# Absolute values on ScalarE instead of VectorE in an encoder layer's sigmoids, softplus and attention

## The chip, the cores and the metric

The kernel runs on one core of one Trainium2 chip. The core has five engines that run side by side, each in its own order of instructions: TensorE (PE in the profile, its weight loads PEld), VectorE (DVE), ScalarE (ACT), GpSimd (POOL) and SyncE (SP), which issues most of the transfers. The metric is the device time of one execution in microseconds, lower is better.

## The reference

One layer of a streaming encoder is applied to 1024 prompt frames and 64 sample frames with the same weights, in fp32. The parts that the change touches are these:

```python
z = jnp.where(mask, jnp.einsum('bhqd,bhnkd->bhqnk', qf[...], ki), SB_NEG)   # attention scores
sp = jax.nn.softplus(z)
c_in = jnp.einsum('bhqnj,js->bhqns', sp, upper)                            # running sums along the keys
a = jnp.exp(z - c_in - later[..., None])                                   # stick-breaking weights
outs.append(jnp.einsum('bhqnk,bhnkd->bhqd', a, vi))

qkv = jax.nn.silu(causal_depthwise(full, conv_w))                          # sigmoids: delta rule, its gate,
a = u[..., :GROUP_W] * jax.nn.sigmoid(u[..., GROUP_W:])                    # conv module (twice),
ffn = (jax.nn.silu(h2 @ ffn_w_gate) * (h2 @ ffn_w_up)) @ ffn_w_down        # feed-forward
g = -jnp.exp(a_log) * jax.nn.softplus(u_a + dt_bias)                       # decays of the delta rule
```

Around them stand a modulation from a condition vector, RMS norms, one input projection, four mixers (a convolution of 31 taps, a gated delta rule in chunks of 64, pooling, attention), an output projection and a SwiGLU feed-forward net.

## The kernel before, in words

The frames are cut into half A (512 prompt frames) and half B (512 prompt frames and the 64 sample frames). Features lie on the 128 partitions, frames along the free dimension. Every large product is done three times with operands that are split into a rounded part and a remainder (`hi`, `lo`, and `whi`, `wlo` for weights): `load_w` fetches a weight tile (`wraw`), ACT rounds it (`whi`, L117), DVE subtracts (`wlo`, L123), and `gemm_fm` issues the matmuls (`pg`, L141). The program is written in this order: `in_proj(HA)`, `mixers(HA)`, `in_proj(HB)`, `mixers(HB)`, `out_proj(HA)`, `ffn(HA)`, `out_proj(HB)`, `ffn(HB)`. A scheduler then lays the instructions of each engine out in a fixed order of its own, from a model of their durations and from priorities, so that one half's matrix products fill in where the other half's mixers wait. A small edit can therefore move instructions of every engine. Each engine then runs its list strictly in order, and an instruction that waits holds up all behind it.

Softplus and sigmoid are built from one table set that has both the exponential and the logarithm: softplus(z) = max(z, 0) + ln(1 + exp(-|z|)). The absolute value is taken by DVE, which clears the sign bit (`vabs`, L134 and L135), then ACT does the exponential and the logarithm (L114), then DVE adds the maximum (L126).

`sb_block` (from L446) handles one block of attention scores, at most 128 keys by 512 queries. There are 16 blocks for half A (4 heads of 4), 32 for half B and 2 for the sample frames. PE writes the scores to the only bank of tag `z`. ACT copies them to `zs` (three buffers), DVE writes their absolute value to `e` (one buffer), ACT does the exponential and the logarithm on `e`, DVE adds the maximum. The sum is split into `sh` (ACT) and `sl` (DVE), PE multiplies both with a triangle (`u_r`) into `psC`, DVE subtracts that from `zs`, ACT takes the exponential, PE adds the other triangle (`omu_r`) to `psC` for the next block and multiplies by the values into `psO`. For half B the weights are split again into `ph` and `pl`.

`sigmoid_chain` (from L183) is used for the delta rule's features and gate (`dne`, `ge`), the convolution's input and output (`cve`, `cvz`), 14 feed-forward tiles of half A (`fe`) and once at the start. The later feed-forward tiles use ACT's Silu, which needs another table set. `dn_decays` has a softplus of its own (`abl`).

`dn_group` (from L702) does four chunks of the delta rule at a time, twice for each half, and once for the sample frames. It begins with `pgcb`, then `pkk` and `pkq` (products of keys and queries); DVE makes `nl` from `pkk`. `nl` goes out to DRAM (`nld`), comes back in another layout (`fsn`), POOL solves triangles of 16 rows (`fst`, `fsu`), the result goes out (`xd`) and comes back as `X`. Only then can PE do the transposes `pw`, and the chain of the four chunks after them.

Of the kernel before, what the change touches and what calls it, by code (L numbers as in the profile page):

```python
# [9 lines left out]
I32 = mybir.dt.int32  # L10
ACTF = mybir.ActivationFunctionType
ALU = mybir.AluOpType
# [47 lines left out]
def hybrid_encoder_kernel(ctx: ExitStack, tc: tile.TileContext, io):  # L60
    nc = tc.nc
# [46 lines left out]
    def PZ(name):  # L108
        return ps_sb.tile([P, 512], F32, tag="z", name=name)
# [3 lines left out]
    def act_(out, in_, func, bias=0.0, scale=1.0):  # L113
        nc.scalar.activation(out, in_, func, bias=bias, scale=scale)  # L114

    def copy_a(out, in_):
        nc.scalar.activation(out, in_, ACTF.Copy)  # L117

    def copy_v(out, in_):
        nc.vector.tensor_copy(out=out, in_=in_)  # L120

    def tt(out, a, b, op):
        nc.vector.tensor_tensor(out=out, in0=a, in1=b, op=op)  # L123

    def stt(out, a, s, b, op0, op1):
        nc.vector.scalar_tensor_tensor(out, a, s, b, op0, op1)  # L126
# [4 lines left out]
        else:  # L131
            nc.vector.tensor_scalar(out, a, s1, s2, op0, op1)

    def vabs(out, a):  # L134
        nc.vector.tensor_scalar(out.bitcast(I32), a.bitcast(I32), 0x7FFFFFFF, None, ALU.bitwise_and)  # L135

    def ptt(out, a, b, op):
        nc.gpsimd.tensor_tensor(out=out, in0=a, in1=b, op=op)  # L138

    def mm(out, lhsT, rhs, start=True, stop=True):  # L140
        return nc.tensor.matmul(out, lhsT=lhsT, rhs=rhs, start=start, stop=stop)  # L141

    def mms(out, lhsT, rhs, start=True, stop=True):
        nc.tensor.matmul(out, lhsT=lhsT, rhs=rhs, start=start, stop=stop, skip_group_check=True)  # L144

    def f(ap):
        return ap.bitcast(F32)
# [7 lines left out]
    def C(name):  # L155
        o, w = CONST_COLS[name]
        return cst[:, o:o + w]

    def V(name, i=None, n=1):
        o, w = VEC_COLS[name]  # L160
        if i is None:
            return vec[:, o:o + w]
        return vec[:, o + i:o + i + n]
# [17 lines left out]


    def sigmoid_chain(e, a):  # L183
        vabs(e, a)
        act_(e, e, ACTF.Exp, scale=-1.0)
        act_(e, e, ACTF.Ln, bias=1.0)
        stt(e, a, 0.0, e, ALU.min, ALU.subtract)
        act_(e, e, ACTF.Exp)
# [8 lines left out]
    def ada_setup():  # L197
        t = sm.tile([P, KT, 2], F32, tag="c2t", name="c2t", bufs=1)
        sigmoid_chain(t, c2)
        tt(c2, c2, t, ALU.mult)  # L200
        cb = [sb.tile([P, 1024], F32, tag=f"cb{g}", name=f"cb{g}") for g in range(2)]
        for g in range(2):
            for x in range(2):
                d = TT("cdiag")[:, 0:512]
                tt(d.rearrange("p (k c) -> p k c", c=P), C("ident").unsqueeze(1).to_broadcast([P, 4, P]),
                   c2[:, 4 * x:4 * x + 4, g:g + 1].to_broadcast([P, 4, P]), ALU.mult)
                pb = PD("pcb")
                mm(pb, C("ones"), d)
                copy_a(cb[g][:, 512 * x:512 * x + 512], pb)
            cbt.append(cb[g])  # L210
# [236 lines left out]
    def sb_block(rows, wid, zmm, psC, psO, kpart, first, last, avs, rounded=True):  # L447
        z = PZ("z")
        zmm(z)
        zs = sb.tile([P, 512], F32, tag="zs", name="zs", bufs=3)  # L450
        e = sb.tile([P, 512], F32, tag="e", name="e")
        r = slice(rows, 128)
        copy_a(zs[r, 0:wid], z[r, 0:wid])
        vabs(e[r, 0:wid], zs[r, 0:wid])
        act_(e[r, 0:wid], e[r, 0:wid], ACTF.Exp, scale=-1.0)
        act_(e[r, 0:wid], e[r, 0:wid], ACTF.Ln, bias=1.0)
        stt(e[r, 0:wid], zs[r, 0:wid], 0.0, e[r, 0:wid], ALU.max, ALU.add)
        sh = sb.tile([P, 512], F32R, tag="sh", name="sh")
        sl = sb.tile([P, 512], F32R, tag="sl", name="sl")
        copy_a(sh[r, 0:wid], e[r, 0:wid])  # L460
        tt(sl[r, 0:wid], e[r, 0:wid], f(sh[r, 0:wid]), ALU.subtract)
        o = 512 - wid if psC is not None and kpart else 0
        mms(psC[:, o:o + wid], u_r[r], sh[r, 0:wid], first, False)
        mms(psC[:, o:o + wid], u_r[r], sl[r, 0:wid], False, False)
        tt(zs[r, 0:wid], zs[r, 0:wid], psC[r, o:o + wid], ALU.subtract)
        act_(zs[r, 0:wid], zs[r, 0:wid], ACTF.Exp)
        if not last:
            mms(psC[:, o:o + wid], omu_r[r], sh[r, 0:wid], False, False)
            mms(psC[:, o:o + wid], omu_r[r], sl[r, 0:wid], False, False)
        if not rounded:  # L470
            for i, (v, out, c0) in enumerate(avs):
                n = out.shape[-1]
                mms(out, v, zs[r, c0:c0 + n], first and i == 0, last)
            return
        ph = sb.tile([P, 512], F32R, tag="ph", name="ph")
        copy_a(ph[r, 0:wid], zs[r, 0:wid])
        pl = sb.tile([P, 512], F32R, tag="pl", name="pl")
        tt(pl[r, 0:wid], zs[r, 0:wid], f(ph[r, 0:wid]), ALU.subtract)
        for i, (v, out, c0) in enumerate(avs):
            n = out.shape[-1]  # L480
            mms(out, v, ph[r, c0:c0 + n], first and i == 0, False)
            mms(out, v, pl[r, c0:c0 + n], False, last)
# [149 lines left out]
    def dn_decays(h):  # L632
        NC = 9 if h.samp else 8
        ab = abt[h.name]
        v = dn.tile([P, 2, 2, 9], F32, tag="abv", name="abv")
        nt = 5 if h.samp else 4
        for par in range(2):
            n_t = nt if par == 1 else 4
            pe = ps_dn.tile([P, 512], F32, tag="dn", name="psel")
            rp = slice(64 * par, 64 * par + 64)  # L640
            mm(pe[:, 0:8 * n_t], C("sel2")[rp], ab[rp, 0:n_t].rearrange("p t c -> p (t c)"))
            src = pe[:, 0:8 * n_t].rearrange("p (t a q b) -> p a q t b", a=2, q=2, b=2)
            for hp in range(2):
                r = slice(64 * hp, 64 * hp + 64)
                for a in range(2):
                    copy_v(v[r, a, :, par:8:2], src[r, a, :, 0:4, hp])
                    if n_t == 5:
                        copy_v(v[r, a, :, 8:9], src[r, a, :, 4:5, hp])
        vv = v[:, :, :, 0:NC]
        tt(vv[:, 0], vv[:, 0], V("dtb").unsqueeze(2).to_broadcast([P, 2, NC]), ALU.add)  # L650
        l = dn.tile([P, 2, 2, 9], F32, tag="abl", name="abl")
        ll = l[:, :, :, 0:NC]
        vabs(ll, vv)
        act_(ll, ll, ACTF.Exp, scale=-1.0)
        act_(ll, ll, ACTF.Ln, bias=1.0)
        D = {}
        for nm in ("g", "lnb", "gc", "kd", "gl", "beg", "beta"):
            D[nm] = dn.tile([P, 2, 9], F32, tag=f"c_{nm}", name=f"c_{nm}")[:, :, 0:NC]
        ea = sm.tile([P, 2], F32, tag="ea", name="ea", bufs=1)
        act_(ea, V("alog"), ACTF.Exp)  # L660
        stt(D["g"], vv[:, 0], 0.0, ll[:, 0], ALU.max, ALU.add)
        stt(D["g"], D["g"], -1.0, ea.unsqueeze(2).to_broadcast([P, 2, NC]), ALU.mult, ALU.mult)
        stt(D["lnb"], vv[:, 1], 0.0, ll[:, 1], ALU.min, ALU.subtract)
        pg = ps_dn.tile([P, 512], F32, tag="dn", name="pgc")
        mm(pg[:, 0:2 * NC], C("bdu"), D["g"])
        mm(pg[:, 64:64 + 2 * NC], C("bdones"), D["g"])
        copy_v(D["gc"], pg[:, 0:2 * NC].rearrange("p (a c) -> p a c", a=2))
        tot = pg[:, 64:64 + 2 * NC].rearrange("p (a c) -> p a c", a=2)
        tt(D["kd"], tot, D["gc"], ALU.subtract)
        act_(D["kd"], D["kd"], ACTF.Exp)  # L670
        act_(D["gl"], tot, ACTF.Exp)
        act_(D["beta"], D["lnb"], ACTF.Exp)
        tt(D["lnb"], D["gc"], D["lnb"], ALU.add)
        act_(D["beg"], D["lnb"], ACTF.Exp)
        D["gcl"] = D["lnb"]
        return D
# [663 lines left out]
def build(nc):  # L1340
    io = {}
    for n, s in _IN_SHAPES:
        io[n] = nc.dram_tensor(f"in_{n}_dram", s, F32, kind="ExternalInput").ap()
    for n, s in _OUT_SHAPES:
        io[n] = nc.dram_tensor(f"out_{n}_dram", s, F32, kind="ExternalOutput").ap()
    with tile.TileContext(nc, schedule_with_timeline_sim=True) as tc:
        hybrid_encoder_kernel(tc, io)
# [10 lines left out]
```

## Time and profile before

| | |
|---|---|
| median of 3 runs | 1543.53 us (1539.69 to 1544.31) |
| the profiled execution, its own time | 1542.9 us |
| its span, first to last instruction | 1541.1 us |
| busy: PE, PEld | 1467.3 us, 1263.4 us |
| busy: DVE, ACT, POOL | 1056.2 us, 626.8 us, 87.4 us |
| mean granted TensorE clock | 0.949 |

The span is cut into stages for reading. A busy time of PE that equals a stage's length means that matmuls follow one another; matmuls are pipelined, so a busy PE need not be at its peak. The granted clock stands as a share of full speed (1.00 is 2.4 GHz). Idle time of an engine is listed with what ended it.

### The profile page before, as it was taken

The page shows a single profiled execution, that of the slowest core. Times are in us where ns is not written, and L with a number is a line of the kernel's source. Part 1 is how long each engine was busy: PE and PEld are TensorE (multiplying, and loading weights), DVE is VectorE, ACT ScalarE, POOL GpSimd, SP SyncE. Part 2 cuts the span into 40 slices and gives each one's busy share as a digit, 9 for nine tenths or more (in the row PEclk, how much of TensorE's full clock was granted, in tenths as well). Part 3 has the DMA queues.
Part 4 walks back from the last instruction along what each step waited for, and adds up shares of the span by engine and source line. Part 5 has one row for each costly group of instructions (what it writes and reads, how often), then busy time and mean ns, then how long its engine had stood idle before and what let it go on. Part 6 is the DMA issues. An engine that isn't in the chain of part 4 may idle for free.

```text
span 1541.1 us, 24527 instructions
## 1 busy us (share of the span) xinstructions
PE 1467.3 (95%) x9688; PEld 1263.4 (82%) x9688; DVE 1056.2 (69%) x1911; ACT 626.8 (41%) x1096; POOL 87.4 (6%) x196
## 2 busy tenths in 40 slices
PE   7999999968998989899999989999999999999999
PEld 5777899745896867587777767789899999999998
DVE  8887799857488998776777588744655455555554
ACT  4446444535543566465566442222432222222221
POOL 0001300030003000300300000000000000000000
PEclk8999799958997999799999999999999999999999
DMA  8787577231555223242323478632322222222222
GB/s 311 274 280 232 168 220 233 98 85 60 166 165 135 70 54 88 83 145 88 101 88 92 131 241 260 216 109 84 127 78 83 83 83 83 83 83 83 83 83 103
DMA packets 106866, 205.40 MB, mean 133 GB/s; under 512 B 39360, under 2 KB 49024, under 8 KB 106752
## 3 DMA queue, kind: packets, MB, share of 16 engines
q1 hardware_dynamic: 99936, 193.36, 39.0%
q0 software_dynamic: 6816, 10.49, 3.0%
q8 instruction: 76, 1.25, 0.3%
q14 instruction: 38, 0.31, 0.1%
HBM read 175.57 MB, written 28.24 MB: 132 GB/s over the span
## 4 chain that ended last, share of the span: by engine, by line
PE 73%; DMA 9%; DVE 9%; issue 3%; ACT 2%; POOL 2%; SPq 2%; DVEq 0%; ACTq 0%; POOLq 0%
PE pg L141 59%; DMA wads<-in_wadat_dram 3%; PE psC L144 2%; DVE junk L215 2%; PE pw L141 1%; PE psO L144 1%; DVE wlo L123 1%; PE z L144 1%; POOL fsu L138 1%; POOL fst L138 1%; DMA nld<-nl 1%; DMA X<-xd 1%; DVE xA L126 1%; DMA wadt<-in_wadat_dram 1%; DVE cy L126 1%
## 5 line engine op out<-in xcount | busy, mean ns | idle before, releaser
L141 PE MATMUL pg<-hi,whi 128*128 128x288 f32 (+1 forms) x1504 | 504.5, 336 | 8.6 <-ACT whi L117 4.2
L141 PE MATMUL pg<-hi,wlo 128*128 128x288 f32 (+1 forms) x1504 | 500.5, 334 | 5.5 <-DVE wlo L123 5.3
L141 PE MATMUL pg<-lo,whi 128*128 128x288 f32 (+1 forms) x1504 | 501.6, 334 | 1.9 <-DVE lo L126 1.9
L117 ACT ACTIVATE whi<-wraw 128x1024 fp32r<-128x1024 f32 (+2 forms) x192 | 199.4, 1040 | 503.2 <-PE pg L141 442.1
L141 PEld LDWEIGHTS pg<-hi,whi 128*128 128x128 f32 x1504 | 286.6, 191 | 37.1 <-ACT whi L117 5.8
L141 PEld LDWEIGHTS pg<-hi,wlo 128*128 128x128 f32 x1504 | 286.3, 190 | 30.4 <-DVE wlo L123 7.6
L141 PEld LDWEIGHTS pg<-lo,whi 128*128 128x128 f32 x1504 | 286.9, 191 | 29.2 <-issue 4.2
L123 DVE TENSOR_TENSOR wlo<-wraw,whi 128x1024 fp32r<-128x1024 f32 (+2 forms) x192 | 230.3, 1200 | 97.6 <-ACT whi L117 95.8
L141 PE MATMUL pg<-g,whi 128*128 128x288 f32 (+1 forms) x1056 | 253.9, 331 | 5.5 <-DVE xA L126 5.0
L141 PEld LDWEIGHTS pg<-g,whi 128*128 128x128 f32 x1056 | 178.5, 189 | 22.8 <-DVE xA L126 6.9
L141 PE MATMUL pg<-g,wlo 128*128 128x288 f32 (+1 forms) x528 | 172.8, 329 | 0.0
L126 DVE SCALAR_TENSOR_TENSOR xs<-pg,mod,xs 128x288 f32<-128x288 f32 (+2 forms) x288 | 106.4, 412 | 85.7 <-PE pg L141 82.6
L141 PEld LDWEIGHTS pg<-g,wlo 128*128 128x128 f32 x528 | 99.6, 189 | 7.8
L123 DVE TENSOR_TENSOR fa<-fa,pg 128x288 f32<-128x288 f32 (+1 forms) x66 | 35.0, 531 | 100.0 <-PE pg L141 96.6
L126 DVE SCALAR_TENSOR_TENSOR cy<-cvb,vec,cy 128x512 f32<-128x512 f32 (+1 forms) x120 | 94.0, 793 | 0.2
L126 DVE SCALAR_TENSOR_TENSOR xA<-pg,mod,xA 128x512 f32<-128x512 f32 x96 | 70.3, 745 | 15.5 <-PE pg L141 15.3
L114 ACT ACTIVATE e<-e 128x512 f32<-128x512 f32 (+4 forms) x100 | 51.5, 515 | 39.0 <-DVE e L135 37.7
L215 DVE CUSTOM_DVE_ANT_0 junk<-wads,cb,vec 128x1024 bf16<-128x1024 f32 x32 | 41.0, 1282 | 14.7 <-DMA wads<-in_wadat_dram 14.5
L141 PE MATMUL pg<-mixs,whi 128*128 128x288 f32 x256 | 50.9, 295 | 0.0
L215 DVE CUSTOM_DVE_ANT_0 junk<-wadt,cb,vec 128x1024 bf16<-128x1024 f32 x32 | 40.9, 1278 | 11.6 <-DMA wadt<-in_wadat_dram 11.6
L141 PEld LDWEIGHTS pg<-mixs,whi 128*128 128x128 f32 x256 | 41.0, 188 | 0.1
L114 ACT ACTIVATE zs<-zs 128x512 f32<-128x512 f32 (+4 forms) x50 | 25.7, 514 | 34.5 <-DVE zs L123 34.4
(305 smaller groups left out, 1920.6 us busy)
## 6 DMA issues: line engine op xcount, KB each, us to landing
wraw<-in_wgate_dram SPq DMA_DIRECT2D x44, 512.0 KB, 3.6
wraw<-in_wup_dram SPq DMA_DIRECT2D x44, 512.0 KB, 3.8
wraw<-in_wdown_dram SPq DMA_DIRECT2D x44, 512.0 KB, 3.7
wadt<-in_wadat_dram SPq DMA_DIRECT2D x32, 512.0 KB, 4.6
wads<-in_wadat_dram SPq DMA_DIRECT2D x32, 512.0 KB, 4.2
wraw<-in_wfm_dram SPq DMA_DIRECT2D x30, 512.0 KB, 4.6
wraw<-in_wout_dram SPq DMA_DIRECT2D x16, 512.0 KB, 3.8
xA<-in_xa_dram SPq DMA_DIRECT2D x16, 256.0 KB, 5.5
```

Of the source, the lines that this page charges most:

```text
L114: nc.scalar.activation(out, in_, func, bias=bias, scale=scale)
L117: nc.scalar.activation(out, in_, ACTF.Copy)
L123: nc.vector.tensor_tensor(out=out, in0=a, in1=b, op=op)
L126: nc.vector.scalar_tensor_tensor(out, a, s, b, op0, op1)
L138: nc.gpsimd.tensor_tensor(out=out, in0=a, in1=b, op=op)
L141: return nc.tensor.matmul(out, lhsT=lhsT, rhs=rhs, start=start, stop=stop)
L144: nc.tensor.matmul(out, lhsT=lhsT, rhs=rhs, start=start, stop=stop, skip_group_check=True)
L215: nc.vector.tensor_tensor_reduce(out=junk, in0=w, in1=cbt[g], scale=1.0, scalar=V("b_ada", col), op0=ALU.mult, op1=ALU.add, accum_out=mod[ ...
```

## The change

Three places take the absolute value with ACT's Abs (by the helper `act_`, L114) instead of DVE's instruction: `sigmoid_chain`, the decays, and the attention. In the attention Abs reads the scores directly from PSUM, and the copy of the scores to `zs` is written behind the logarithm instead of in front of everything. `vabs` is gone, so the lines behind it have numbers smaller by three.

```diff
-    def vabs(out, a):
-        nc.vector.tensor_scalar(out.bitcast(I32), a.bitcast(I32), 0x7FFFFFFF, None, ALU.bitwise_and)
-
...
     def sigmoid_chain(e, a):
-        vabs(e, a)
+        act_(e, a, ACTF.Abs)
         act_(e, e, ACTF.Exp, scale=-1.0)
         act_(e, e, ACTF.Ln, bias=1.0)
         stt(e, a, 0.0, e, ALU.min, ALU.subtract)
...
         r = slice(rows, 128)
-        copy_a(zs[r, 0:wid], z[r, 0:wid])
-        vabs(e[r, 0:wid], zs[r, 0:wid])
+        act_(e[r, 0:wid], z[r, 0:wid], ACTF.Abs)
         act_(e[r, 0:wid], e[r, 0:wid], ACTF.Exp, scale=-1.0)
         act_(e[r, 0:wid], e[r, 0:wid], ACTF.Ln, bias=1.0)
+        copy_a(zs[r, 0:wid], z[r, 0:wid])
         stt(e[r, 0:wid], zs[r, 0:wid], 0.0, e[r, 0:wid], ALU.max, ALU.add)
...
-        vabs(ll, vv)
+        act_(ll, vv, ACTF.Abs)
         act_(ll, ll, ACTF.Exp, scale=-1.0)
```

The scheduler lays the program out anew. ACT, at the first attention blocks of half A (`zs` is the copy of the scores, `e` the block's softplus; the other names are other mixers' and projections' tiles). Before:

```order
L117 ACTIVATE zs_2410<-z_2406 128x128
L114 ACTIVATE cve_2835<-cve_2835 128x512
L117 ACTIVATE Y_1603<-pw0_1650 128x512
L117 ACTIVATE zs_2432<-z_2428 128x256
L117 ACTIVATE zs_2454<-z_2450 128x384
L114 ACTIVATE dne_1920<-dne_1920 128x512
L117 ACTIVATE vf_3031<-pv_2981 128x264
L114 ACTIVATE e_2411<-e_2411 128x128
```

Now:

```order
L114 ACTIVATE e_2411<-z_2406 128x128
L117 ACTIVATE zs_2410<-z_2406 128x128
L114 ACTIVATE cve_2835<-cve_2835 128x512
L114 ACTIVATE e_2411<-e_2411 128x128 x2
L117 ACTIVATE Y_1603<-pw0_1650 128x512
```

Before, three blocks' copies stood ahead of the first block's exponential. Now each block's Abs and copy stand as a pair, and the next block's pair comes after the exponential and logarithm of this one.

PE, at the second chunk group of half A, in front of the transposes of the solved triangle (`pw`); `psC` and `psO` are the attention's sums and outputs, `pvar` belongs to the convolution. Before:

```order
L141 MATMUL pvar<-cvs,cst 128x256 x2
L144 MATMUL psO<-zs,v_2594 64x256
L144 MATMUL psC<-sh,u_r 128x384
L144 MATMUL psC<-sl,u_r 128x384
L141 MATMUL pvar<-cvs,cst 128x256 x2
L731 MATMUL pw_2130<-cst,X 64x64
```

Now:

```order
L141 MATMUL psC<-sl,u_r 128x384
L141 MATMUL z<-q_2693,k_2691 128x128 x2
L141 MATMUL z<-neg_r,id_r 128x128
L141 MATMUL psC<-sh,omu_r 128x384
L141 MATMUL psC<-sl,omu_r 128x384
L141 MATMUL psO<-zs,v_2594 64x384
L141 MATMUL psC<-sh,u_r 128x512
L141 MATMUL psC<-sl,u_r 128x512
L728 MATMUL pw_2130<-cst,X 64x64
```

The rest of the 384-wide block and the first two matmuls of the 512-wide block now stand in front of `pw`; before they stood behind it.

DVE, at the first chunk group of half B, from the first tap of the convolution (`cy0`) to `nl`, which starts the way of the triangle through DRAM and POOL. Before:

```order
L132 TENSOR_SCALAR cy0_6808<-cvb_6793,vec_106 128x606
L126 SCALAR_TENSOR_TENSOR cy0_6808<-cvb_6793,vec_106,cy0_6808 128x606 x2
L123 TENSOR_TENSOR wlo_4322<-wraw_4319,whi_4321 128x1024
L126 SCALAR_TENSOR_TENSOR cy0_6808<-cvb_6793,vec_106,cy0_6808 128x606 x2
L120 COPY cvb_6842<-cvcar_126 128x30
L126 SCALAR_TENSOR_TENSOR cy0_6808<-cvb_6793,vec_106,cy0_6808 128x606 x2
L135 TENSOR_SCALAR cve_6841<-cvg_6840 128x576
L126 SCALAR_TENSOR_TENSOR cy0_6808<-cvb_6793,vec_106,cy0_6808 128x606 x2
L123 TENSOR_TENSOR wlo_7055<-wraw_7052,whi_7054 128x1024
L126 SCALAR_TENSOR_TENSOR cy0_6808<-cvb_6793,vec_106,cy0_6808 128x606
L126 SCALAR_TENSOR_TENSOR cve_6841<-cvg_6840,cve_6841 128x576
L126 SCALAR_TENSOR_TENSOR nl_4529<-pkk_4512,W_4506 128x512
```

Now:

```order
L132 TENSOR_SCALAR cy0_6808<-cvb_6793,vec_106 128x606
L126 SCALAR_TENSOR_TENSOR cy0_6808<-cvb_6793,vec_106,cy0_6808 128x606 x2
L123 TENSOR_TENSOR wlo_4322<-wraw_4319,whi_4321 128x1024
L126 SCALAR_TENSOR_TENSOR cy0_6808<-cvb_6793,vec_106,cy0_6808 128x606
L120 COPY cvb_6842<-cvcar_126 128x30
L126 SCALAR_TENSOR_TENSOR nl_4529<-pkk_4512,W_4506 128x512
```

`nl` stood behind ten steps of the convolution and two instructions of a sigmoid (`cve`); now it stands behind four steps, and the sigmoid's absolute value is no longer on DVE.

## Rows read from the trace of the kernel before

**Rows 1.** The page: busy us (share of the span) and instructions; granted clock in 40 slices.
```profile
PE 1467.3 (95%) x9688; PEld 1263.4 (82%) x9688; DVE 1056.2 (69%) x1911; ACT 626.8 (41%) x1096; POOL 87.4 (6%) x196
...
PEclk8999799958997999799999999999999999999999
```
**Rows 2.** Table by stage: window, busy us (instructions) of each engine, clock, DMA.
```profile
core 0: us, PE busy (x) PEld busy (x) DVE busy (x) ACT busy (x) POOL busy (x), PEclk, DMA share, GB/s
305.00:400.00 95.00, 73.08 (x588) 49.42 (x589) 57.33 (x128) 42.17 (x93) 15.28 (x37) 0.77 0.30 83
450.00:550.00 100.00, 92.42 (x668) 71.45 (x666) 92.22 (x151) 44.35 (x79) 14.50 (x34) 0.86 0.42 118
550.00:640.00 90.00, 80.10 (x440) 59.02 (x440) 78.56 (x155) 54.05 (x101) 11.89 (x32) 0.88 0.25 67
1140.00:1240.00 100.00, 100.00 (x757) 100.00 (x756) 52.46 (x103) 23.37 (x31) 0.00 (x0) 1.00 0.27 85
```
**Rows 3.** PE's waits: for whom, us in total, times, longest us.
```profile
PE pw L731 <- DMA X<-xd: 11.2, 3, 5.2
PE psC L144 <- DVE zs L123: 8.0, 6, 3.5
...
PE z L144 <- ACT zs L117: 4.1, 3, 2.4
```
**Rows 4.** Groups by form: busy us, mean ns of one, idle before it; 512-wide.
```profile
L114 ACT ACTIVATE e<-e 128x512 f32<-128x512 f32 x48 | 30.1, 627 | 19.3 <-DVE e L135 18.6
L117 ACT ACTIVATE sh<-e 128x512 fp32r<-128x512 f32 x24 | 15.1, 628 | 11.6 <-PE psC L144 7.9 <-DVE e L126 2.7 <-PE po L144 0.6
L117 ACT ACTIVATE zs<-z 128x512 f32<-128x512 f32 x24 | 14.1, 588 | 12.1 <-DVE pl L123 9.3 <-PE psO L144 2.0 <-PE z L144 0.8
L123 DVE TENSOR_TENSOR sl<-e,sh 128x512 fp32r<-128x512 f32 x24 | 16.7, 695 | 5.1 <-ACT sh L117 5.1
L126 DVE SCALAR_TENSOR_TENSOR e<-zs,e 128x512 f32<-128x512 f32 x24 | 16.5, 686 | 7.6 <-ACT e L114 7.6
L135 DVE TENSOR_SCALAR e<-zs 128x512 int32<-128x512 int32 x24 | 10.1, 420 | 0.3
```
**Rows 5.** Line 135: who waited for it (us, times).
```profile
  ACT e L114: 37.7, 25
  ACT fe L114: 10.6, 9
```
**Rows 6.** PE in order of time at half A's second group: start us, us, what [idle].
```profile
340.90 0.28 PE L731 MATMUL pw<-cst,X 64*64 64x64 f32 x1 [5.22 <-DMA X<-xd]
343.51 0.47 PE L141 MATMUL pw<-cst,X 64*64 64x64 f32 x2 [2.33 <-DMA X<-xd]
...
348.44 0.69 PE L144 MATMUL psC<-sh,omu_r 128*128 128x384 f32 x1
...
349.37 1.54 PE L144 MATMUL psO<-zs,v 128*64 128x384 f32 x2
```
**Rows 7.** PE and DVE in order of time at half B's first group.
```profile
443.13 0.45 PE L141 MATMUL pkk<-dnf 64*64 64x64 f32 x8
...
450.20 0.22 PE L141 MATMUL pkk<-dnf 64*64 64x64 f32 x1
...
451.82 0.68 DVE L126 SCALAR_TENSOR_TENSOR nl<-pkk,W 128x512 f32<-128x512 f32 x1
...
485.06 0.31 PE L731 MATMUL pw<-cst,X 64*64 64x64 f32 x1 [4.91 <-DMA X<-xd]
```
**Rows 8.** DVE and PE in order of time, before half A's down projection resumes.
```profile
632.80 0.42 DVE L135 TENSOR_SCALAR e<-zs 128x512 int32<-128x512 int32 x1
...
634.73 0.73 PE L141 MATMUL pg<-g,whi 128*128 128x512 f32 x2 [2.23 <-DVE xA L126]
```
**Rows 9.** PE in order of time: the longest wait for the score bank.
```profile
361.48 0.73 PE L144 MATMUL z<-q,k 128*128 128x512 f32 x2 [2.44 <-ACT zs L117]
```
**Rows 10.** Table by stage of `sl` alone: busy us of PE, PEld, DVE (x blocks).
```profile
305.00:400.00 95.00, 5.94 (x14) 3.56 (x14) 3.98 (x8) 0.77 0.30 83
450.00:640.00 190.00, 8.16 (x22) 4.43 (x22) 6.39 (x11) 0.87 0.34 94
```

## The prediction

> **What bounds the kernel now.** I read the page's shares first, then the stages one by one, then TensorE's waits. TensorE (PE) is busy 95% of the span, VectorE (DVE) 69%, ScalarE (ACT) 41% [rows 1]. That PE share is not one limit for the whole program. The table by stage [rows 2] shows PE at 100 of 100 us with a granted clock of 1.00 between 1140 and 1240 us; there, nothing that another engine saves can end the program sooner. It is different in three stretches: 305 to 400 us (PE 73.08 of 95 us, clock 0.77), 450 to 550 (92.42 of 100, clock 0.86) and 550 to 640 (80.10 of 90, clock 0.88). In them PE waits 39.4 us in sum, and a low clock is granted besides. In 450 to 550 DVE is busy 92.22 of 100 us. What there is to gain lies in these stretches, and it must come from PE waiting less.
>
> What does PE wait for? Its own list of waits [rows 3] has, of what this change can touch, `pw` waiting for the DMA of `X` (11.2 us in 3 waits, the solved triangle coming back to the delta rule), `psC` waiting for DVE's `zs` (8.0 us in 6), and the score matmul `z` waiting for ACT's copy of the scores before (4.1 us in 3).
>
> **What is removed and added.** 95 DVE instructions at L135 go: 50 in the attention (one per score block), 42 in sigmoids, 2 in the decays, 1 at the start. A 512-wide one takes 420 ns [rows 4], so at most 95 x 0.42 = 39.9 us of DVE time goes. In their place ACT gets 95 Abs. In the sigmoids and decays they read SBUF, and cost what ACT's Exp in place costs at the same width, 627 ns; in the attention they read PSUM, where the copy of the same scores takes 588 ns [rows 4]. At most 95 x 0.627 = 59.6 us, on an engine that is busy 626.8 of 1541.1 us [rows 1]. In most stages both are beside the path: the cover is PE's unbroken stream of matmuls, and without it ACT would be 59.6 us longer and DVE 39.9 us shorter. The table loads stay five in the listings of both kernels, in the same places around the Silu, so no set is changed for Abs; they are costed at nothing.
>
> What the hop cost is seen from its other end: ACT stood idle 37.7 us in 25 waits for the attention's absolute value and 10.6 us in 9 for the FFN's [rows 5]. This is ACT's idle time, not PE's, and I count none of it directly.
>
> **The moved copy.** The source puts the copy of the scores behind the logarithm. The listing of the changed ACT queue has it directly behind Abs in 49 of the 50 blocks, so it is not later in fact: Abs and copy both stand in front of Exp. In the kernel before, ACT copied scores up to two blocks ahead (three copies, 128, 256 and 384 wide, before the first Exp is done); now Abs writes `e`, of which there is one buffer, so it waits for the block before to finish its `sl` on DVE. This holds the one score bank longer, and behind the waiting Abs stand the weight roundings (`whi`) that PE's next tiles need.
>
> **The path, term by term.** Four terms; each is bounded from both sides.
>
> (a) 305 to 400 us. In the second chunk group of half A, PE finishes `pvar` and then waits 5.22 and 2.33 us for `X` before the transposes `pw` [rows 6]. In the new listing, the rest of the 384-wide block (two `omu` matmuls and `psO`) and the first two of the 512-wide block stand ahead of `pw` instead of behind it. Behind it they cost PE, before, 348.44 to 350.91 = 2.5 us, and the two `u` matmuls I price like the `omu` pair beside them, 0.9 us (348.44 to 349.37). Put into the wait they are free: -3.4 us. At the least 0, if DVE delivers `zs` too late for them; at the most -7.6, the whole wait.
>
> (b) 450 to 550 us. The first group of half B: PE stands 4.91 us before `pw` until `X` is there at 485.06 [rows 7]. The chain starts with `nl` on DVE at 451.82, right behind the last `pkk` matmul (450.20 to 450.42). In the new listing all 16 `pkk` are out one weight tile earlier: before, the third batch ended at 443.13 + 0.45 = 443.58, so `nl` may start up to 6.8 us sooner, and on DVE it stands behind four steps of the convolution instead of ten. What follows, 33.2 us from `nl` to `X`, is POOL's and the queues' own. 6.8 us is more than the wait: -4.9 us. Bounds 0 and -4.9; I take the full size, since the shift exceeds the wait by 1.9 us.
>
> (c) 550 to 640 us. The second wait of PE for DVE's residual `xA` is 2.23 us [rows 8]; in front of it on DVE stands one 420 ns absolute value that goes. Earlier ones are followed by idle time of DVE (it is free 11.4 of 90 us here [rows 2]) and so are absorbed. -0.4 us, between 0 and -2.2.
>
> (d) Where PE waits for the score bank, the bank is now held for an Abs besides the copy: three waits [rows 3], the longest 2.44 us [rows 9], each longer by 0.588: +1.8 us, between 0 and that.
>
> Sum: -3.4 - 4.9 - 0.4 + 1.8 = -6.9 us. The profiled execution took 1542.9 us by its own time (span 1541.1 and 1.8 around it), 0.6 below the median of the three runs, 1543.5. 1542.9 - 6.9 = 1536.0, and on the median's footing **1536.6 us**. With each term at its ends (-7.6, -4.9, -2.2, 0 and 0, 0, 0, +1.8) this case gives 1528.8 to 1545.3.
>
> **Rivals.** *All of it is covered.* PE's order changes little: the matmuls and their number are the same, and PE is 95% busy. If `X` comes back as late as before relative to PE (POOL's solve and two trips through DRAM set that, and neither is touched), (a) and (b) shrink to nothing and the time stays within 1540 to 1547, about 1543. For it: `X` is 33 us of latency, and DVE's 40 us are mostly in full stretches. Against: the listing does move `nl`.
>
> *ACT becomes the late one, slower.* This is the mechanism on the other side. One 512-wide block's trip over `e` was, before, absolute value 0.420, Exp and Ln 2 x 0.627, maximum 0.686, rounding 0.628, `sl` 0.695 = 3.7 us [rows 4]; now 0.420 gives way to Abs and copy, 2 x 0.588, so 0.76 us more per block, and nothing runs ahead of it. Price: the three stretches that are not full hold 8 + 11 blocks, counted by their `sl` [rows 10]; at full size 19 x 0.76 = 14 us, and as half of them are narrower than 512, near 11. It decides if PE's matmuls of the next block stand right behind the last ones of this block, as at the 2.44 us wait [rows 9]; then (a) and (b) are eaten up and 1543.5 + 4 to 11 gives 1547 to 1555, say 1552. Against it: 8 blocks in 95 us is one every 12 us, so a loop of 3.7 + 0.76 us has room.
> The Trainium skill, "ScalarE: Activation LUTs", section "Rules for kernel authors", says that operations such as maximum, add and multiply belong on VectorE rather than ScalarE. By that rule the change is a loss, and the trace agrees for the single instruction (420 against 588 to 627 ns); by it the sum would be that of this rival.
>
> *More than the sum.* If the extra matmuls fill all of PE's waits in (a), 1527 or less: -7.6 - 4.9 - 2.2 = -14.7, and a stretch of clock 0.77 that is granted more.
>
> **How the numbers follow.** Forecast 0.50 (of it 0.42 below 1539, 0.08 above), covered 0.22 (0.19 unchanged, 0.03 slower), late ACT 0.20, more than the sum 0.08. A change of 0.3%, 4.6 us, is about what a measurement of this kernel can tell from none. Faster than 1538.9: 0.42 + 0.08 = 0.50. Within: 0.08 + 0.19 = 0.27. Slower than 1548.1: 0.20 + 0.03 = 0.23. The range leaves out half of the late ACT and the tail of the last case: 1526 to 1551.
>
> **What would show it.** After: no L135 group; DVE near 1020 us, ACT near 680 us; PE before the second `pw` of half A waits under 4 us, and before the first of half B not at all; the stage 305 to 400 shortened by about 3 us and everything behind it moved forward; PE's waits for ACT's `zs` at `z` by about 2 us longer. Wrong it is if `X` still ends PE's wait at (b), if PE's new waits are for ACT's `e` or `sh`, if `whi` appears behind Abs as a wait of more than some us, or if the gain at 400 us is lost again before 1000 us, where the loads for half B's modulation fill the DMA queues.

## The result and the profile after

The changed kernel took 1528.87 us in the median of four runs (1522.53 to 1532.56) beside 1543.92 us for the kernel before on the same chip (1539.69 to 1551.15): a ratio of 0.9891 with a 95% interval of 0.9861 to 0.9922. It is faster by 15 us, a little more than twice the forecast of 6.9 us, inside the range given and close to the third rival's 14.7 us. The direction was forecast; the size and, as will be seen, most of the places were not.

The page of its profiled execution (1532.56 us by its own time, span 1530.8 us), the rows that answer to [rows 1]:

```profile
PE 1459.6 (95%) x9688; PEld 1259.9 (82%) x9688; DVE 1030.5 (67%) x1816; ACT 663.2 (43%) x1191; POOL 88.3 (6%) x196
...
PEclk7999999968897999699999999999999999999999
```

DVE has 95 instructions and 25.7 us less, ACT 95 instructions and 36.4 us more. Both are under the ceilings of 39.9 and 59.6 us, since half of the blocks are narrower than 512. PE does the same 9688 matmuls in 7.7 us less of busy time and is idle for 71.2 us (span less busy) instead of 73.8. So 2.6 of the 10.3 us between the two spans are waiting; three quarters are matmuls that take less long.

PE's waits, which answer to [rows 3] (for whom, us in total, times, longest us):

```profile
PE pw L728 <- DMA X<-xd: 13.8, 2, 10.3
PE pqk L138 <- ACT qksq L114: 5.8, 4, 2.7
...
PE psC L141 <- ACT sh L117: 3.4, 4, 2.0
...
PE psC L141 <- DVE sl L123: 2.5, 2, 1.9
...
PE psC L141 <- DVE zs L123: 2.0, 4, 0.8
...
PE z L141 <- ACT zs L117: 1.4, 1, 1.4
```

Against before: `X` 13.8 instead of 11.2 us (16.1 instead of 14.5 with the transposes of L138, which was L141 before), `zs` at the running sum 2.0 instead of 8.0, the score bank 1.4 instead of 4.1. New or longer are `qksq` (5.8), `sh` and `sl`. Waits for the residual `xA`, of which one is in [rows 8], are gone from the list.

The new instructions cost what they were priced at ([rows 4] had 588 and 627 ns). ACT by form, 512-wide (busy us, mean ns of one | idle before it):

```profile
L114 ACT ACTIVATE e<-e 128x512 f32<-128x512 f32 x48 | 30.3, 632 | 0.3
...
L117 ACT ACTIVATE zs<-z 128x512 f32<-128x512 f32 x24 | 14.2, 592 | 0.0
L114 ACT ACTIVATE e<-z 128x512 f32<-128x512 f32 x24 | 14.2, 591 | 8.7 <-DVE sl L123 8.6
```

ACT's idle time before the exponential fell from 19.3 to 0.3 us, and 8.7 us of it came back before Abs, which waits for `sl` to leave the one buffer `e`, as forecast.

**Where the time came from.** Five first matmuls of groups cut the program into stretches. PE in order of time, before:

```profile
292.81 0.59 PE L141 MATMUL pgcb<-W,cst 128*128 128x512 f32 x1
...
367.97 0.37 PE L141 MATMUL pu<-vb,Y 64*64 64x64 f32 x2
...
421.43 0.59 PE L141 MATMUL pgcb<-W,cst 128*128 128x512 f32 x1
...
529.47 0.33 PE L141 MATMUL pu<-vb,Y 64*64 64x64 f32 x4
...
739.41 0.38 PE L141 MATMUL pgcb<-W,cst 128*128 128x128 f32 x2
```

After:

```profile
295.10 0.59 PE L138 MATMUL pgcb<-W,cst 128*128 128x512 f32 x1
...
364.18 0.39 PE L138 MATMUL pu<-vb,Y 64*64 64x64 f32 x6
...
421.63 0.59 PE L138 MATMUL pgcb<-W,cst 128*128 128x512 f32 x1
...
526.66 0.33 PE L138 MATMUL pu<-vb,Y 64*64 64x64 f32 x4
...
729.30 0.39 PE L138 MATMUL pgcb<-W,cst 128*128 128x128 f32 x2
```

With a second profile of the changed kernel (the first experiment) beside it, the lengths of the stretches in us are as follows. The scheduler moves some matmuls across these cuts, so a shorter stretch is not a gain by itself; PE's idle time in it (length less busy time) and its number of matmuls stand beside it. Each cell has before, after, and after again; the number of matmuls in S2 to S6 is the same in both profiles after.

| stretch | length | PE idle | matmuls |
|---|---|---|---|
| S1: start to `pgcb` of half A's second group | 292.8, 295.1, 295.9 | 16.7, 18.6, 18.2 | 1803, 1821, 1822 |
| S2: to its `pu` (holds term (a)) | 75.2, 69.1, 71.8 | 19.3, 20.0, 21.7 | 411, 400 |
| S3: to `pgcb` of half B's first group | 53.5, 57.4, 56.0 | 3.6, 7.4, 5.8 | 432, 424 |
| S4: to its `pu` (holds term (b)) | 108.0, 105.0, 104.7 | 5.9, 4.4, 4.1 | 718, 719 |
| S5: to `pgcb` of the sample group (holds term (c)) | 209.9, 202.6, 195.8 | 11.6, 8.0, 8.0 | 1343, 1316 |
| S6: to the end | 801.7, 801.5, 802.5 | 16.8, 12.9, 13.1 | 4989, 5015 |

S5 and S6, before and then after (window, its length, busy us and instructions of PE, PEld, DVE, ACT and POOL, clock, DMA):

```profile
529.47:739.41 209.94, 198.31 (x1343) 151.00 (x1343) 164.27 (x295) 122.32 (x231) 17.72 (x42) 0.92 0.31 90
739.41:1541.10 801.69, 784.93 (x4989) 719.31 (x4987) 472.51 (x818) 256.51 (x384) 18.99 (x42) 0.99 0.36 114
```

```profile
526.66:729.30 202.64, 194.68 (x1316) 146.59 (x1316) 153.71 (x263) 130.26 (x255) 15.81 (x42) 0.91 0.31 89
729.30:1530.80 801.50, 788.60 (x5015) 724.71 (x5013) 469.03 (x799) 267.73 (x412) 20.22 (x42) 1.00 0.36 114
```

The lengths of S2 and S4 change by about what (a) and (b) said, but PE's idle time does not fall in S2; it rises, and in S3 it rises more. It falls by 1.5 and 1.7 us in S4. The largest falls are in S5, 3.7 us, where the prediction had 0.4, and in S6, 3.9 and 3.7 us, where it had nothing: S6 keeps its length because it now holds 26 matmuls more. S5 is shorter by 7.3 and 14.2 us, and a part of this is work that left it, 27 matmuls.

### The profile page after: what moved, and what is told of

Same layout as the page of the kernel before. It is cut to its first block, busy times and chain, and to the rows that moved or that the text cites. A ratio compares the mean times of both kernels' runs of the same rounds, so it can differ in the third digit from the quotient of the medians.

```text
span 1530.8 us, 24538 instructions
## 1 busy us (share of the span) xinstructions
PE 1459.6 (95%) x9688; PEld 1259.9 (82%) x9688; DVE 1030.5 (67%) x1816; ACT 663.2 (43%) x1191; POOL 88.3 (6%) x196
## 4 chain that ended last, share of the span: by engine, by line
PE 70%; issue 11%; DMA 7%; DVE 6%; POOL 3%; ACT 2%; SPq 1%; DVEq 0%; POOLq 0%; ACTq 0%
PE pg L138 59%; PE psC L141 2%; POOL fst L135 1%; POOL fsu L135 1%; PE pw L138 1%; DVE junk L212 1%; PE psO L141 1%; PE z L141 1%; DVE wlo L123 1%; DMA out_sbk_dram<-qk 1%; DMA wadt<-in_wadat_dram 1%; DMA X<-xd 1%; DMA fsn<-nld 1%; DVE xA L126 1%; DVE nrm L126 1%
## 5 line engine op out<-in xcount | busy, mean ns | idle before, releaser
L138 PE MATMUL pg<-hi,whi 128*128 128x288 f32 (+1 forms) x1504 | 504.8, 336 | 7.6 <-ACT vf L117 3.3
L138 PE MATMUL pg<-hi,wlo 128*128 128x288 f32 (+1 forms) x1504 | 500.6, 334 | 4.8 <-DVE wlo L123 4.8
L138 PE MATMUL pg<-lo,whi 128*128 128x288 f32 (+1 forms) x1504 | 502.5, 334 | 1.7 <-DVE lo L126 1.6
L138 PEld LDWEIGHTS pg<-hi,whi 128*128 128x128 f32 x1504 | 287.1, 191 | 35.5 <-ACT vf L117 4.1
L138 PEld LDWEIGHTS pg<-hi,wlo 128*128 128x128 f32 x1504 | 286.4, 191 | 29.9 <-DVE wlo L123 6.8
L138 PEld LDWEIGHTS pg<-lo,whi 128*128 128x128 f32 x1504 | 287.2, 191 | 27.9 <-issue 3.3
L138 PE MATMUL pg<-g,whi 128*128 128x288 f32 (+1 forms) x1056 | 253.1, 332 | 0.1
L138 PEld LDWEIGHTS pg<-g,whi 128*128 128x128 f32 x1056 | 180.0, 190 | 14.8 <-ACT acc L114 0.6
L138 PE MATMUL pg<-g,wlo 128*128 128x288 f32 (+1 forms) x528 | 173.1, 331 | 0.0
L138 PEld LDWEIGHTS pg<-g,wlo 128*128 128x128 f32 x528 | 100.1, 190 | 7.8
L114 ACT ACTIVATE e<-e 128x512 f32<-128x512 f32 (+4 forms) x100 | 51.9, 519 | 0.8
L212 DVE CUSTOM_DVE_ANT_0 junk<-wadt,cb,vec 128x1024 bf16<-128x1024 f32 x32 | 41.0, 1282 | 16.3 <-DMA wadt<-in_wadat_dram 16.2
L138 PE MATMUL pg<-mixs,whi 128*128 128x288 f32 x256 | 50.9, 295 | 0.0
L114 ACT ACTIVATE zs<-zs 128x512 f32<-128x512 f32 (+4 forms) x50 | 25.7, 514 | 36.8 <-DVE zs L123 35.7
L138 PEld LDWEIGHTS pg<-mixs,whi 128*128 128x128 f32 x256 | 41.0, 188 | 0.1
```

The lines of the kernel that those rows point to most:

```text
L212: nc.vector.tensor_tensor_reduce(out=junk, in0=w, in1=cbt[g], scale=1.0, scalar=V("b_ada", col), op0=ALU.mult, op1=ALU.add, accum_out=mod[ ...
```

## The experiments

Each kernel was profiled, and timed beside the kernel before in five rounds (the first row of the changed one is the result above). All results first; ratios are to the kernel before, with 95% intervals, idle is span less PE's busy time, and the last column adds PE's waits that are put down to DVE.

| kernel | median us | ratio | span | PE busy | PE idle | for DVE |
|---|---|---|---|---|---|---|
| before | 1544 to 1547 | 1 | 1541.1 | 1467.3 | 73.8 | 28.6 |
| after (first profile) | 1528.87 | 0.9891 (0.9861 to 0.9922) | 1530.8 | 1459.6 | 71.2 | 20.7 |
| after, again | 1531.79 | 0.9896 (0.9856 to 0.9935) | 1526.7 | 1455.7 | 71.0 | 22.2 |
| sigmoids only | 1550.83 | 1.0025 (1.0000 to 1.0049) | 1550.1 | 1478.1 | 72.0 | 33.3 |
| attention only | 1559.31 | 1.0085 (1.0055 to 1.0114) | 1564.2 | 1479.3 | 84.9 | 36.4 |
| copy first | 1534.77 | 0.9916 (0.9885 to 0.9948) | 1537.3 | 1468.1 | 69.2 | 26.9 |
| before, other heads | 1550.57 | 1.0044 (1.0022 to 1.0066) | 1549.3 | 1469.1 | 80.2 | 40.5 |
| after, other heads | 1534.04 | 0.9945 (0.9925 to 0.9964) | 1530.7 | 1457.8 | 72.9 | 27.0 |
| before, other pooling | 1564.01 | 1.0135 (1.0113 to 1.0157) | 1563.6 | 1476.6 | 87.0 | 36.2 |
| after, other pooling | 1544.28 | 0.9994 (0.9969 to 1.0018) | 1542.4 | 1460.3 | 82.1 | 28.4 |
| DVE's work put back | 1553.56 | 1.0070 (1.0040 to 1.0100) | 1560.5 | 1478.5 | 82.0 | 28.4 |
| the same, other heads | 1547.67 | 1.0031 (1.0006 to 1.0056) | 1543.9 | 1461.8 | 82.1 | 31.5 |
| sigmoids only, other heads | 1541.62 | 0.9987 (0.9964 to 1.0011) | 1536.0 | 1460.3 | 75.7 | 36.7 |
| attention only, other heads | 1550.70 | 1.0026 (1.0002 to 1.0050) | 1549.4 | 1473.9 | 75.5 | 25.8 |

Three theories stood at the start: the relief of DVE (theory 1), the order that the scheduler happens to lay out (theory 2), and the attention's new way of reading scores (theory 3).

**The change once more.**

> The changed kernel once more, for a second profile and a tighter ratio. Ratio to before 0.989 +-0.003 by every theory. If the 4.7 us by which the first profile of the changed kernel lay behind the kernel before at 125 us is scatter of the transfers at the start, it is under 2 us here, and the first gate matmul of the delta rule's second group (295 us) comes 2 us or more earlier than in the kernel before; if it is the change's own, it comes back at 4 to 5 us.

The ratio held. The first `pgcb` (half A's first group, 125.0 us before) comes 2.6 us late in the second profile instead of 4.7, between the two values expected, and over all profiles of this study it lies between 124.1 and 129.6 us, with the change and without; this is scatter of the start. The one of the second group, however, came at 295.9, no earlier than before (292.8): this expectation failed, and S1 is not shorter.

**The two halves alone.** The sigmoids:

```diff
     def sigmoid_chain(e, a):
-        vabs(e, a)
+        act_(e, a, ACTF.Abs)
...
-        vabs(ll, vv)
+        act_(ll, vv, ACTF.Abs)
```

> Only the sigmoids (42), decays (2) and the start (1) take their absolute value on ACT; the attention is that of the kernel before. Theory 1 (every absolute value that leaves DVE shortens what waits for DVE; 45 of 95 go, most of them in stretches where PE is full anyway): between 1536 and 1542, a third of the gain or less. Theory 2 (the gain is the scheduler's new order, whichever edit brings it): anywhere between 1527 and 1550, with no relation to the number of instructions moved. Theory 3 (the attention's new way of reading scores brings the gain): no change, 1540 to 1545.

The attention (its part of the change alone, `vabs` kept for the rest):

```diff
-        copy_a(zs[r, 0:wid], z[r, 0:wid])
-        vabs(e[r, 0:wid], zs[r, 0:wid])
+        act_(e[r, 0:wid], z[r, 0:wid], ACTF.Abs)
         act_(e[r, 0:wid], e[r, 0:wid], ACTF.Exp, scale=-1.0)
         act_(e[r, 0:wid], e[r, 0:wid], ACTF.Ln, bias=1.0)
+        copy_a(zs[r, 0:wid], z[r, 0:wid])
```

> Only the attention's 50 blocks are changed (Abs on ACT from the score bank, copy written behind Ln); sigmoids stay on DVE. Theory 1: 1530 to 1536, two thirds of the gain, and with the sigmoids' kernel the two gains add to about 15 us. Theory 2: anywhere between 1527 and 1550; the two gains do not add. Theory 3: the whole gain, 1527 to 1531.

Each half alone is slower than the kernel before, by 4 us (at the edge of its interval) and 13 us, and both together are 15 us faster. Theories 1 and 3 had them at 1536 to 1545 and 1527 to 1536. Theory 2's range, 1527 to 1550, missed both as well, by 0.8 and 9.3 us; what it had right is that the two do not add. In the attention-only profile PE waits for `X` at four groups (half A's second, both large ones of half B, the sample group), and once for DVE's `sbo`, at 936 us, ahead of half A's deferred down projection:

```profile
PE pw L731 <- DMA X<-xd: 20.2, 4, 6.5
PE pg L141 <- DVE sbo L123: 7.4, 1, 7.4
```

The second wait also stands in both reorderings of the kernel before, below (7.8 and 7.6 us), which have nothing of the change, and in the changed kernel with the other pooling (7.8). So it comes with an order and not with the change, as theory 2 would have it.

**The copy in front.**

```diff
-        act_(e[r, 0:wid], z[r, 0:wid], ACTF.Abs)
+        copy_a(zs[r, 0:wid], z[r, 0:wid])
+        act_(e[r, 0:wid], zs[r, 0:wid], ACTF.Abs)
         act_(e[r, 0:wid], e[r, 0:wid], ACTF.Exp, scale=-1.0)
         act_(e[r, 0:wid], e[r, 0:wid], ACTF.Ln, bias=1.0)
-        copy_a(zs[r, 0:wid], z[r, 0:wid])
```

> The changed kernel, but the copy of the scores is written first and Abs reads the copy in SBUF: the same 95 instructions on ACT, the score bank is held for the copy alone. Theory 1: 1526 to 1531, as the change. Theory 2: anywhere between 1522 and 1545. Theory 3 (reading from the bank matters): back to 1540 or above; if the bank's being held longer is a cost instead, 1 to 2 us below the change, with PE's waits of the score matmul for the copy shorter than 1.4 us.

It keeps most of the gain, so theory 3 fell: reading the scores from PSUM is not what the change is worth. Its 1534.8 us lie above theory 1's 1526 to 1531 and inside theory 2's range. PE's waits of the score matmul fell to 0.2 us, and yet the kernel is not faster than the change, so holding the bank longer is no cost that shows. Its S5 is 208.1 us, almost that of before. It holds 1345 matmuls again, and waits like those that vanished there are back:

```profile
631.46 0.73 PE L138 MATMUL pg<-g,whi 128*128 128x512 f32 x2 [2.48 <-DVE xA L126]
...
639.21 0.21 PE L728 MATMUL pw<-cst,X 64*64 64x64 f32 x1 [3.10 <-DMA X<-xd]
```

So single waits come and go with the order; the ratio moved from 0.9896 to 0.9916.

**Neutral reorderings, in pairs.** To size what order alone does, the same two swaps, which change no work, were made in both kernels:

```diff
-        for hd in range(4):
+        for hd in (1, 0, 3, 2):
```

> The kernel before, with the attention's heads taken in the order 1, 0, 3, 2: the same work, only the scheduler lays out another order (1109 lines of PE's list differ; 976 between the kernel before and the changed one). Theory 1 (the change's gain is its own, worth about 15 us in any order; the single parts lost because their order happened to be bad): within 5 us of the kernel before or not, but its partner with the change is 10 to 20 us faster than it. Theory 2 (the time follows the order that the scheduler happens to lay out, of which the change is one throw): it lies 5 to 15 us off the kernel before, on either side, and the pair's difference may have either sign.

> The changed kernel with the heads in the order 1, 0, 3, 2. Theory 1: 10 to 20 us below the kernel before with the same order of heads. Theory 2: between 1525 and 1560, with no fixed distance to its partner.

and, in `pool`,

```diff
-        for i in range(2):
+        for i in (1, 0):
```

> The kernel before, with the two halves of the pooling taken in the order 1, 0: the same work again, another order on every engine (996 lines of PE's list differ). Theory 1 and theory 2 as for the kernel before with other heads.

> The changed kernel with the two halves of the pooling taken in the order 1, 0. Theory 1: 10 to 20 us below its partner. Theory 2: between 1525 and 1560, with no fixed distance to its partner.

Order alone is worth up to 19 us: the kernel before goes from about 1545 to 1550.6 and 1564.0, the changed one from about 1530 to 1534.0 and 1544.3. But each pair keeps its distance: 0.9896, 0.9945 / 1.0044 = 0.9901 and 0.9994 / 1.0135 = 0.9861. That is 15 to 20 us each, inside theory 1's 10 to 20. By theory 2 the sign was open; two further pairs with the same sign and nearly the same size speak against it for the change as a whole, and the 19 us of the other pooling are also more than the 5 to 15 us that it named. Over the whole table, every kernel with both halves of the change and without DVE's work put back is faster than all others with the same order of heads and pooling. Three orders are few, and this is likely rather than certain. What theory 2 says of size holds for every single kernel: a difference of 1% between two kernels with different orders can be the order's alone. The pages of the pair with other heads, before and after:

```profile
PE 1469.1 (95%) x9688; PEld 1262.4 (81%) x9688; DVE 1057.0 (68%) x1911; ACT 626.1 (40%) x1096; POOL 87.2 (6%) x196
```

```profile
PE 1457.8 (95%) x9688; PEld 1253.9 (82%) x9688; DVE 1028.7 (67%) x1816; ACT 661.9 (43%) x1191; POOL 93.0 (6%) x196
```

In each pair PE's busy time falls by 8 to 16 us, its idle time by 2.6 to 7.3, and its waits for DVE by 6 to 14 us, whichever waits these are. Where the time goes differs: with other heads S6 becomes 16.3 us shorter (822.1 to 805.8 us, 39 matmuls fewer) and S1 11.6 us longer (43 more). PE's idle time in S5 falls in all three pairs, by 3.7, 1.9 and 5.2 us.

**DVE's work put back, without the hop.** The hop is the trip of ACT's chain over DVE for the absolute value.

```diff
+    def vand(a):
+        nc.vector.tensor_scalar(a.bitcast(I32), a.bitcast(I32), -1, None, ALU.bitwise_and)
...
     def sigmoid_chain(e, a):
         act_(e, a, ACTF.Abs)
+        vand(a)
...
         copy_a(zs[r, 0:wid], z[r, 0:wid])
+        vand(zs[r, 0:wid])
```

> The changed kernel with DVE's work put back, but not the hop: 93 neutral instructions (a bitwise and with all ones, in place, of the kind and width of the absolute values that went: 50 on the copied scores, 42 on the sigmoids' inputs, 1 at the start), beside ACT's Exp and Ln, which do not wait for them. Theory 1a (the gain is DVE's queue being 25 us shorter): back to 1543 to 1553, with PE's waits for DVE at 28 us or more in sum. Theory 1b (the gain is that ACT's chain no longer goes over DVE): stays at 1525 to 1538, with PE's waits for DVE between 20 and 28 us. Theory 2 (order alone): anywhere from 1525 to 1560.

> The same with the heads in the order 1, 0, 3, 2, whose partners took 1550.6 (before) and 1534.0 (changed). Theory 1a: 1547 to 1556. Theory 1b: 1530 to 1540. Theory 2: anywhere, and not on the same side as in the usual order of heads.

In both orders the gain is gone: 1.0070 against 0.9891 to 0.9896 for the change, 1.0031 against 0.9945. Theory 1a held in time (the first is half a microsecond over its range); theory 2's 1525 to 1560 holds both times too. PE's waits for DVE are at 28.4 and 31.5 us, as theory 1a asked, but the changed kernel with the other pooling has 28.4 as well, so this sum alone decides nothing. PE's idle time, 82.0 and 82.1 us, is above that of the kernel before in either order (73.8 and 80.2). The page, two waits and DVE's neutral instruction (busy us, mean ns | idle before it):

```profile
PE 1478.5 (95%) x9688; PEld 1267.9 (81%) x9688; DVE 1055.9 (68%) x1909; ACT 662.9 (42%) x1191; POOL 90.9 (6%) x196
```

```profile
PE pw L733 <- DMA X<-xd: 19.6, 4, 5.1
PE psC L144 <- DVE sl L123: 9.1, 6, 3.8
```

```profile
L135 DVE TENSOR_SCALAR zs<-zs 128x512 int32<-128x512 int32 x24 | 10.2, 427 | 7.1 <-ACT zs L117 7.0
```

DVE's busy time is that of before (1055.9 and 1056.2 us). One thing differs: DVE also stands idle in front of the neutral instruction, 7.1 us for the 512-wide ones, where before it was 0.3 [rows 4], and 18.3 us over all 93. Part of that is a wait that DVE has in any case: in front of the attention's maximum it waits 18.1 us for ACT in the changed kernel and 4.5 here. The rest holds DVE's queue more than the work alone would. So the losses of 1.8% (1.0070 / 0.9896) and 0.9% (1.0031 / 0.9945) may be more than DVE's 25 us cost by themselves; the pairs' 1.0 to 1.4% lie between them. Order alone moved the kernel before by 0.4 and 1.35%, so two orders make DVE's load the likeliest cause and do not settle its size. Against the kernel before, this kernel has the hop removed and ACT's 36 us added, at DVE's old load: 1.0070 in one order and 1.0031 / 1.0044 = 0.9987 in the other. The removal of the hop shows no gain of its own in these two orders.

**The halves in the other order of heads.** The same edits as above with the heads swapped; "theory 3" in these texts is that the halves help only together.

> Only sigmoids and decays on ACT, heads in the order 1, 0, 3, 2. Theory 1 (each part has a gain of its own, which a bad order hid in the first pair): between its partners, 1537 to 1547. A theory 3 that the parts help only together: 1550 or above, as the kernel before with these heads. Theory 2: 1535 to 1565, unrelated to the first.

> Only the attention changed, heads in the order 1, 0, 3, 2. Theory 1: between its partners, 1535 to 1545, a larger share of the gain than the sigmoids'. Theory 3: 1550 or above. Theory 2: 1535 to 1565, unrelated to the first (1559.3).

The sigmoids alone now gain 9 us on their partner (1541.62 and 1550.57), as theory 1 said; the attention alone gains nothing (1550.70), as theory 3 said. Theory 2's 1535 to 1565 holds both and told little. Over both orders the sigmoids' half lost 4 us and gained 9, the attention's half lost 13 and 0, though the attention's half takes more off DVE (13.7 us of busy time against 11.6). Nor do PE's waits for DVE put the two in order: 25.8 us in the attention's half, the slower one, and 36.7 in the sigmoids'. Why the attention's half earns nothing until the sigmoids' half is there stays open, and with it how DVE's load turns into time. A second buffer for `e`, which would let Abs run ahead, and each half in more orders were not tried.

## Why the prediction was right and where it was not

The direction was right, and the idea behind it, that less work on DVE makes PE wait less, is what the experiments make likely. That the time lies inside the range is in part luck: term (a) saved no waiting, (b) gave two thirds or less of its size, (c) nine times its size, (d) has the wrong sign, and most of the gain came by the clock, which is not in the sum. Two of the four signs that the prediction named for being wrong are there: `X` still ends PE's wait at (b), and PE has new waits for `sh`. A third, the loss of the gain at 400 us, is there in part (S3). `whi` did not become one (2.2 us of waits instead of 4.2).

**(a), 305 to 400 us, -3.4: the length is near, by luck; the reading of the wait is not right, and most of it was lost again.** S2 became shorter by 6.1 and 3.4 us, but PE's idle time in it grew by 0.7 and 2.4. What fell is work, 11 matmuls, and time at the low clock (below). PE's wait for `X` did not shrink either; it grew from 5.22 and 2.33 [rows 6] to

```profile
341.39 0.31 PE L728 MATMUL pw<-cst,X 64*64 64x64 f32 x1 [10.32 <-DMA X<-xd]
343.79 0.47 PE L138 MATMUL pw<-cst,X 64*64 64x64 f32 x2 [2.08 <-DMA X<-xd]
```

`X` comes at nearly the same time as before, 0.5 us later; PE has done the attention's matmuls by then, and has them no longer to do behind `pw`. The forecast of a wait under 4 us mistook work that is pulled ahead for a wait that is filled. S3 then gave back 4.0 and 2.6 us; PE's idle time in it grew by 3.8 and 2.2, most of it in waits for ACT that were 1.4 us in sum before:

```profile
382.14 1.32 PE L138 MATMUL pqk<-qksq,cst 128*128 128x288 f32 x2 [1.56 <-ACT qksq L114]
...
398.93 1.33 PE L138 MATMUL pqk<-qksq,cst 128*128 128x288 f32 x2 [2.72 <-ACT qksq L114]
```

This is the rival of the late ACT in small, at a tile that the prediction did not name.

**(b), 450 to 550 us, -4.9: -3.0 and -3.3, of it 1.5 and 1.7 in idle time.** The step that failed is "33.2 us from `nl` to `X` is POOL's and the queues' own", and so fixed. `nl` did move, by more than said, from 451.82 [rows 7] to 443.81, and PE still waits for `X`:

```profile
443.81 0.69 DVE L126 SCALAR_TENSOR_TENSOR nl<-pkk,W 128x512 f32<-128x512 f32 x1 [0.34 <-PE pkk L138]
```

```profile
482.03 0.24 PE L728 MATMUL pw<-cst,X 64*64 64x64 f32 x1 [3.49 <-DMA X<-xd]
```

From `nl` to `pw` it is 38.2 us now. SP's queue shows where 2.9 of the 5 us went; before, the last of the four `fsn` issues came 2.3 us behind the first, with two prefetches of the output projection (`wraw`, `mixt`) in between:

```profile
458.66 1.31 SPq L786 DMA_DIRECT2D fsn<-nld  x3
...
460.98 0.43 SPq L786 DMA_DIRECT2D fsn<-nld  x1
```

and now it comes 5.2 us behind, with four of these prefetches in between, one of which stands for 1.77 us:

```profile
449.53 0.81 SPq L783 DMA_DIRECT2D fsn<-nld  x2
...
450.87 0.43 SPq L783 DMA_DIRECT2D fsn<-nld  x1
451.35 1.77 SPq L1049 DMA_DIRECT2D mixt<-mixA  x1
453.16 0.43 SPq L321 DMA_DIRECT2D wraw<-in_wout_dram  x1
453.64 1.07 SPq L1049 DMA_DIRECT2D mixt<-mixA  x2
454.75 0.43 SPq L783 DMA_DIRECT2D fsn<-nld  x1
```

POOL's solve adds 1.6 us (464.92 to 479.28 before, 458.80 to 474.79 now) and the way from `xd` to `X` 1.3 (3.2 and 4.5 us between their issues); the way from `nl` to the first `fsn` issue gives 1.1 back (6.8 and 5.7 us). An earlier start on DVE was in part spent in queues.

**(c), 550 to 640 us, -0.4: the step that failed most; PE's idle time in S5 fell by 3.7 us.** "Earlier ones are followed by idle time of DVE and so are absorbed" priced one absolute value in front of one wait. Both waits for `xA`, 2.75 and 2.23 us, are gone (the upper bound of 2.2 us was for the second alone), with the wait for `X` behind them; what is left at that place is

```profile
629.65 0.54 PE L141 MATMUL psO<-ph,v 128*128 128x512 f32 x1 [1.41 <-ACT ph L117]
630.92 0.79 PE L141 MATMUL psC<-sh,u_r 128*128 128x512 f32 x1 [0.73 <-ACT sh L117]
```

In the stretch around it, before and then in the two profiles after, PE's idle time falls from 6.9 to 2.3 us (with 946 and 928 matmuls):

```profile
582.50:728.30 145.80, 138.91 (x946) 106.30 (x945) 107.48 (x199) 83.07 (x155) 15.16 (x38) 0.92 0.34 99
```

```profile
579.50:720.20 140.70, 138.37 (x928) 105.08 (x927) 99.14 (x176) 89.11 (x173) 13.44 (x38) 0.89 0.35 100
```

```profile
581.20:715.10 133.90, 131.56 (x928) 100.85 (x927) 99.07 (x176) 88.96 (x173) 13.47 (x38) 0.95 0.37 105
```

**(d), the score bank, +1.8: the wrong sign.** The waits at `z` fell from 4.1 to 1.4 us and those for `zs` from 8.0 to 2.0, while those for `sh` and `sl` rose from 1.2 to 5.9 us. The bank is held for an Abs more. That DVE's instructions, which end a block, come sooner and outweigh this is a reading that no run separates.

**What the sum left out.** All four terms were waits. PE's waits gave 2.6 and 2.8 us of the two profiles' 10.3 and 14.4. The rest is busy time, and in these profiles it is clock: PE's busy time, multiplied by what the granted clock lacks of 1 and added up over stretches of 4 us, makes 67.8 us before, 59.9 and 53.8 after, and 77.4 with DVE's work put back. Taken off the busy time it leaves 1399.4, 1399.7, 1401.9 and 1401.0 us: the same work. In these four profiles the whole change of PE's busy time is time at the lower of its two levels (1.2 of 2.4 GHz). The profiled execution with DVE's work put back took 1562.28 us, 8.7 more than its median, so its 77.4 is high. In the pair with other heads only half of PE's saved busy time is clock, 5.5 of 11.3 us. The mean clock goes from 0.949 to 0.953 and 0.956 in the profiles. Over all executions it was 0.947 to 0.948 before and 0.955 with the change, 0.949 and 0.955 with other heads, 0.943 and 0.952 with the other pooling. In S2, the stretch with the long `X` wait, the lost clock is about 16 us before and 12 after in all three pairs. Many low stretches stand around PE's waits: 340 to 350 us, behind the first `X` wait, was granted 0.50, both before and after. Not all do: before, 460 to 470 us was granted 0.55 with PE busy throughout. The Trainium skill, "TensorE: Matmul & The Clock Gate", section "HAM oscillation — how this bites in real kernels", counts such a penalty beside the waits for data; the traces agree, and in these profiles the penalty saved (7.9 and 14.0 us) is larger than the waits saved. The prediction named it only in the third rival.

**The rivals.** "All of it is covered" fell. "ACT becomes the late one" is there in small, 4.4 us at `qksq` and 2.2 at `sh`. The rule behind it, from the Trainium skill, "ScalarE: Activation LUTs", section "Rules for kernel authors", that operations such as maximum, add and multiply belong on VectorE, does not list the absolute value. Stretched to it, the rule agrees with the single instruction (420 ns on DVE, 591 to 632 on ACT) and not with the kernel's time. The Trainium skill's page "Perfetto Trace Analysis", section "Optimizing Scalar/DVE Operations", has the other side, that work may go to ScalarE where VectorE is saturated; in 450 to 550 us DVE was busy 92.22 of 100 [rows 2]. "More than the sum" has the right time by other terms.

## What to carry to other kernels

Where PE is full on average but waits in stretches, one wait followed by hand says little, since waits change places; pricing an engine's relief by its whole queue in those stretches, and adding what PE's clock loses around the waits, is the better attempt, though nothing here tested it ahead of a result. Where a scheduler lays out the order, make the same neutral swaps in both kernels before an edit worth a per cent is judged, and above all before half of it is. A start that is moved ahead on one engine must be followed through the queues behind it, the DMA issues included.

## What was not expected

The same program was granted different clocks in two executions. In the stretch shown above, 928 matmuls with 2.3 us of idle time took 138.37 us at 0.89 in one profile and 131.56 us at 0.95 in the other. That is 6.8 us of scatter with no wait to point at, in a kernel whose runs spread over 16 us (1523.25 to 1539.27). And a swap of two loops that changes no work cost the kernel before 1.35% (1.13 to 1.57).
